# Two layers of a diffusion backbone on one core: another order of the expert blocks, and another end of the program

## The chip, the core and the metric

The kernel runs on one core of a Trainium2 chip. The core has five engines with a queue of instructions each: TensorE (PE, matmuls), VectorE (DVE), ScalarE (ACT), GpSimd (POOL) and SyncE (SP), which here issues the loads of the weights. They work on an on-chip memory (SBUF) and on eight banks in which matmuls sum (PSUM), and wait for each other through semaphores. The metric is the time of one execution in microseconds; the time of a kernel is the median of its runs.

## The reference

Two layers work on 256 latent tokens and 256 context tokens of width 1024, in float32. Each layer has a mixer (a gating MLP, a Fourier mix and windowed attention side by side) and a channel mixer. The first layer's channel mixer is a dense SwiGLU; the second layer's, for the 256 latent tokens alone, picks two of eight experts per token. This part is what the change is about:

```python
def moe_swiglu(y, w_r, b_r, wg, wu, wd):
    logits = (y @ w_r).astype(jnp.float32) + b_r.astype(jnp.float32)
    top_val, top_idx = lax.top_k(logits, TOP_K)
    gates = jax.nn.softmax(top_val, axis=-1)
    combine = jnp.sum(jax.nn.one_hot(top_idx, N_EXPERTS, dtype=jnp.float32)
                      * gates[..., None], axis=-2).astype(y.dtype)
    out = jnp.zeros_like(y)
    for e in range(N_EXPERTS):
        out = out + combine[..., e:e + 1] * swiglu(y, wg[e], wu[e], wd[e])
    return out
```

Behind it come a normalization of the sum, a multiplication by a gate and the addition to the tokens. Each expert has three matrices of 1024 x 3584, 44 MB in float32.

## The kernel before

The program is recorded by a planner in Python (`Sched`, L92). Work is written as tasks that yield an engine, the buffers they need and the events they wait for; at each step the planner takes the task that could start first by its own table of costs, and records its instructions. So the order on each engine, and the buffer that each tile gets, are fixed when the program is built. On the chip each engine runs its list in order.

In the expert stage a *unit* is one expert with a fixed number of token slots. Unit 0 is expert 0 with 32 slots (L44). The other seven experts are ranked on the chip by how many tokens chose them, and rank r gets `SLOTS[r]` slots: 160, 96, 96, 64, 64, 64, 32. Their weights are loaded through registers that hold the expert's number. An expert that gets more tokens than its unit has slots is served again by up to five overflow passes, each inside a branch (`moe_over`, L1639); the count of passes needed is read into a register of each engine. With the inputs at hand none is needed: the page of the profile lists 224 loads of each of the three kinds of expert weights, 28 for each of eight experts.

A unit has seven blocks of 512 hidden columns (`EB`). A block has 12 loads of 512 KB: four each of gate, up and down weights. The order of units and blocks is a table (L68); an entry is a rank (None for expert 0), the first block and the block behind the last:

```python
SEQ = ((None, 0, 7), (1, 0, 7), (3, 0, 7), (0, 0, 7), (4, 0, 7), (2, 0, 7), (5, 0, 7), (6, 0, 7))
```

`experts` (L1486) goes through it. `parts` (L1480) cuts a unit's slots into 128 rows, where there are so many, and a rest of 64 and 32. The 160-slot unit is the only one with a 128-row part. That part multiplies three times with weights that ScalarE and VectorE have split into a high and a low tile (`t_hi`, `t_lo`, `t_egu`, `t_edown`); the rests multiply with the loaded tile itself (`t_xgu`, `t_xdown`). Gathered tokens meet gate and up weights (128x512, 64x256 or 32x128 outputs), VectorE multiplies the two, TensorE transposes the product, and it meets the down weights (128x512, 64x512 or 32x512 outputs), whose sum stays in PSUM over all blocks of an entry of the table. Then a *flush* (`t_finish`, `t_xfinish`) splits the sum, multiplies it with the tokens' one-hot matrix and adds it, weighted, to two tiles `facc` of 128 tokens each.

Loads, split tiles and other tiles of this size share 41 slots of SBUF. The loads (`t_load`, L378) run ahead of TensorE as far as slots are free, less a reserve for everything that is no load. The reserve is a table too (L53): it starts at 8, and each pair sets it when the loads reach that block of the stage, counted from 0:

```python
REST = (8, ((20, 17), (27, 8)))
```

The unit of rank 0 holds blocks 21 to 27 of the stage. After the last unit's flush all engines meet the branch, and `fin` (L1866) takes the sum of squares of `facc` on ScalarE, multiplies `facc` by the gate on VectorE, and writes the result. All recorded instructions stand under L232 of the profile, the loads under L397, the branch under L1647.

Of the kernel before, what the change touches and what calls it, by code (L numbers as in the profile page):

```python
# [26 lines left out]
NE = 8  # L27
# [3 lines left out]
EPS = 1e-6  # L31
# [18 lines left out]
TABLE = 1.3  # L50
SC = {'PE': 1.0, 'ACT': 1.0, 'DVE': 1.0, 'POOL': 0.918, 'DMA': 1.0, 'NONE': 1.0}

REST = (8, ((20, 17), (27, 8)))  # L53
ORD = ((1, 0, 5, 6, 7, 4, 3, 2, 8, 9, 10, 11), (5, 3, 2, 4, 6, 7, 9, 10, 8, 11, 0, 1))
CAP = (3, 1, 2, 4)
ADB, HI0 = -0.7, 5
# [8 lines left out]
JO = (3, 6, 1, 2, 5, 7, 4, 0)  # L65
WO = ((0, 2), (0, 1, 2, 3), (0, 1, 2, 3, 4, 6))

SEQ = ((None, 0, 7), (1, 0, 7), (3, 0, 7), (0, 0, 7), (4, 0, 7), (2, 0, 7), (5, 0, 7), (6, 0, 7))  # L68


PE, ACT, DVE, POOL, DMA, NONE = "PE", "ACT", "DVE", "POOL", "DMA", "NONE"
# [214 lines left out]
class Core:  # L286
# [1159 lines left out]
            self.sc.rel(ht)  # L1446
        self.sc.set(out, acc)

    def t_finish(self, comb, acc, oht, last):

        fs = yield on(ACT, "sr:fs", "sr:fs", ev=[acc])
        for hf in range(2):
            c = slice(hf * 512, hf * 512 + 512)
            yield from self.g_split(acc.v[hf], fs[0][:, c], fs[1][:, c])
        self.sc.rel(*acc.v)
        yield on(PE, ev=[oht, self.combed, self.faccev])
        comb = comb()
        for t in range(2):
            for hf in range(2):
                c = slice(hf * 512, hf * 512 + 512)  # L1460
                p = yield on(PE, "b:m")
                o = oht.v[:, t * 128:t * 128 + 128]
                self.pe.matmul(p, o, fs[0][:, c], start=True, stop=False)
                self.pe.matmul(p, o, fs[1][:, c], start=False, stop=True)
                yield on(DVE)
                f = self.facc[t][:, c]
                self.v.scalar_tensor_tensor(f, p, comb[:, t:t + 1], f, op0=OP.mult, op1=OP.add)
                self.sc.rel(p)
        self.sc.rel(*fs)
        if last:  # L1470
            self.sc.rel(oht.v)
# [14 lines left out]
    def experts(self, units, seq):  # L1486
# [3 lines left out]
        for key, b0, b1 in seq:  # L1490
# [3 lines left out]
            for s, ws in parts:  # L1494
# [7 lines left out]
                acc = [Event() for _ in ws or [128]]  # L1502
                down.append((self.t_xdown(key, b0, b1, ws, hts, acc) if ws else self.t_edown(key, b0, b1, hts, acc[0]), 0.0))
                for i, w in enumerate(ws or [128]):
                    down.append(((self.t_xfinish if w == 64 else self.t_finish)(comb, acc[i], out[1][i], b1 == EB), -0.2))
            for b in range(b0, b1):
                for s, ws in parts:
                    out, hts = state[key, s]
# [130 lines left out]
    def moe_over(self):  # L1639

        tc, nc = self.tc, self.nc
        novf = nc.values_load(self.onum[0:1, MORE:MORE + 1], min_val=0, max_val=MORE)
        oidx = [nc.values_load(self.onum[0:1, i:i + 1], engines=(mybir.EngineType.SP,), min_val=0, max_val=NE - 1)
                for i in range(MORE)]

        def more(i):
            with tc.If(novf > i):  # L1647
                key = NE + i
                self.stream(self.moe_items([(key, 0, EB)], oidx[i]))
                self.experts({key: (key, lambda: self.otab[:, i, 0:2], 128, 128, lambda: self.otab[:, i, 2:4])}, [(key, 0, EB)])  # L1650
                self.sc.run()
                if i < MORE - 1:
                    more(i + 1)

        more(0)
# [209 lines left out]

    def fin(self):  # L1866

        def t():
            G, o = self.gate[1, 5, 0].v, []

            def mid():
                for t in range(2):
                    o.append((yield on(DVE, "s")))
                    self.v.tensor_mul(o[t], self.facc[t], G)

            rs = yield from self.g_rstd([[self.facc[t]] for t in range(2)], (), mid())
            for t in range(2):
                for hf in range(2):
                    c = slice(hf * 512, hf * 512 + 512)
                    self.v.scalar_tensor_tensor(o[t][:, c], o[t][:, c], rs[:, t:t + 1], self.h[t][:, c], op0=OP.mult, op1=OP.add)  # L1880
                    self.nc.sync.dma_start(self.out[t * 128:t * 128 + 128, c], o[t][:, c])

        self.sc.spawn(t())
        self.sc.run()


# [98 lines left out]
```

## Times and profile before

| | |
|---|---|
| median of three runs | 1733.65 us (1732.76 to 1735.01) |
| the profiled execution | 1729.91 us |
| its span, first to last instruction | 1728.0 us |
| TensorE busy | 1641.0 us (95%), 13276 matmuls |
| VectorE, ScalarE busy | 762.5 us (44%), 532.1 us (31%) |
| read from memory | 494.5 MB, 287 GB/s over the span |
| granted TensorE clock, mean | 0.982 |

The profile is of one execution, and its times are in microseconds from the span's start. The shares of the whole span mix stages: the first half computes the two mixers, the dense channel mixer and the router, and the expert stage runs from about 860 to 1715. The views used below are the slices of the span, stretches with the busy time of each engine and the rate of the loads, the waits of the queue that issues the loads, single instructions in order of time, and the instructions of one line.

### The profile page before, as it was taken

How to read it: one execution, taken by the hardware profiler on the slowest of the kernel's cores; microseconds unless marked ns; L12 is line 12 of the kernel's file. 1: busy time of each engine (PE TensorE's matmuls, PEld its weight loads, DVE VectorE, ACT ScalarE, POOL GpSimd, SP SyncE). 2: the span in 40 equal slices, each digit the busy share in tenths (PEclk: the TensorE clock that was granted, in tenths of full speed). 3: DMA queues.
4: the chain of work that ended last, by engine and by line, in shares of the span. 5: the costliest groups of instructions: out<-in, count | busy, mean ns of one | idle time of the engine just before them, and what ended most of it. 6: DMA issues, size and time to landing. Idle time of an engine off the chain costs nothing. (4 is left out here: it accounts for less than half of the span.)

```text
span 1728.0 us, 33043 instructions
## 1 busy us (share of the span) xinstructions
PE 1641.0 (95%) x13276; PEld 1144.2 (66%) x13276; DVE 762.5 (44%) x1402; ACT 532.1 (31%) x933; POOL 26.1 (2%) x49
## 2 busy tenths in 40 slices
PE   6999999999999999999989999999999999999865
PEld 3776889888888888886755555567776556545331
DVE  4566687664545467986313002165564010020102
ACT  3486453222223245547210001154452000000001
POOL 0100000000000020000000000000000000000000
PEclk9999999999999999999899999999999999999997
DMA  9506445644544465771899999999879999999995
GB/s 382 197 25 245 169 134 197 201 159 152 171 159 164 164 229 197 288 290 40 313 412 412 412 412 413 414 354 337 309 270 383 412 412 411 410 413 413 412 409 224
DMA packets 137888, 497.78 MB, mean 288 GB/s; under 512 B 16348, under 2 KB 16480, under 8 KB 137728
## 3 DMA queue, kind: packets, MB, share of 16 engines
q1 hardware_dynamic: 135072, 490.79, 74.6%
q0 software_dynamic: 1792, 4.18, 0.8%
q8 instruction: 106, 1.74, 0.4%
q10 hardware_dynamic: 864, 0.62, 0.1%
q14 instruction: 54, 0.44, 0.1%
HBM read 494.49 MB, written 1.05 MB: 287 GB/s over the span
## 5 line engine op out<-in xcount | busy, mean ns | idle before, releaser
L232 PE MATMUL b<-s,s 128*128 128x512 f32 (+3 forms) x6056 | 870.5, 344 | 9.6 <-DVE s L232 7.9
L232 PEld LDWEIGHTS b<-s,s 128*128 128x128 f32 (+2 forms) x6056 | 664.0, 157 | 182.5 <-issue 42.7
L232 PE MATMUL b<-s,f 128*32 128x128 f32 (+5 forms) x5472 | 526.9, 358 | 44.2 <-DMA s<-in_w_up_e_dram 12.5
L232 PEld LDWEIGHTS b<-s,f 128*32 128x32 f32 (+2 forms) x5472 | 321.2, 130 | 221.0 <-issue 84.1
L232 DVE TENSOR_TENSOR s<-s,s 128x1024 fp32r<-128x1024 f32 (+2 forms) x253 | 302.6, 1216 | 71.6 <-ACT s L232 56.4
L232 ACT ACTIVATE s<-s 128x1024 fp32r<-128x1024 f32 (+1 forms) x259 | 266.6, 1052 | 186.3 <-PE b L232 112.3
L232 DVE TENSOR_TENSOR f<-f,b 128x256 f32<-128x256 f32 (+3 forms) x91 | 39.1, 430 | 506.4 <-PE b L232 505.0
L232 ACT ACTIVATE f<-b 128x512 f32<-128x512 f32 (+3 forms) x161 | 77.8, 484 | 465.1 <-PE b L232 455.9
L232 PE MATMUL b<-s,q 128*32 128x512 f32 (+2 forms) x720 | 157.9, 592 | 3.2 <-DMA s<-in_w_down_e_dram 2.3
L232 DVE SCALAR_TENSOR_TENSOR s<-s,cs,s 128x1024 f32<-128x1024 f32 x73 | 91.8, 1280 | 42.6 <-DMA s<-in_w_ada_dram 42.5
L232 ACT ACTIVATE q<-b 128x128 f32<-128x128 f32 (+2 forms) x53 | 18.1, 342 | 275.1 <-PE b L232 263.8
L232 PEld LDWEIGHTS b<-s,q 128*32 128x32 f32 (+2 forms) x720 | 42.8, 128 | 74.0 <-issue 44.5
L232 DVE TENSOR_TENSOR s<-b,s 128x512 fp32r<-128x512 f32 (+2 forms) x77 | 48.6, 633 | 62.2 <-ACT s L232 38.4
L232 PE MATMUL b<-ident,f 128*128 128x128 f32 x313 | 57.5, 294 | 12.5 <-DVE f L232 7.8
L232 PEld LDWEIGHTS b<-ident,f 128*128 128x128 f32 x313 | 35.6, 144 | 50.4 <-DVE f L232 28.7
L232 ACT ACTIVATE s<-b 128x512 f32<-128x512 f32 (+3 forms) x99 | 50.2, 528 | 52.2 <-PE b L232 50.7
L232 ACT ACTIVATE f<-f 128x256 fp32r<-128x256 f32 x28 | 11.7, 419 | 116.3 <-DVE f L232 116.3
L232 DVE TENSOR_TENSOR f<-b,f 128x512 fp32r<-128x512 f32 x5 | 3.5, 692 | 89.7 <-ACT f L232 89.7
L232 PEld LDWEIGHTS b<-q,h 128*128 128x128 f32 x288 | 35.5, 201 | 9.3 <-issue 4.5
L232 PE MATMUL b<-q,h 128*128 128x64 f32 (+3 forms) x288 | 37.9, 288 | 1.9 <-DVE q L232 1.9
L232 DVE SCALAR_TENSOR_TENSOR s<-b,utab,s 128x512 f32<-128x512 f32 x40 | 28.5, 746 | 18.1 <-PE b L232 18.1
L232 ACT ACTIVATE f<-b,cols 128x256 f32<-128x256 f32 (+1 forms) x56 | 26.0, 555 | 33.5 <-PE b L232 29.9
(153 smaller groups left out, 560.4 us busy)
## 6 DMA issues: line engine op xcount, KB each, us to landing
s<-in_w_gate_e_dram SPq DMA_DIRECT2D x224, 512.0 KB, 10.0
s<-in_w_up_e_dram SPq DMA_DIRECT2D x224, 512.0 KB, 10.0
s<-in_w_down_e_dram SPq DMA_DIRECT2D x224, 512.0 KB, 10.0
s<-in_w_ada_dram SPq DMA_DIRECT2D x96, 512.0 KB, 4.5
s<-in_w_down_d_dram SPq DMA_DIRECT2D x56, 512.0 KB, 4.2
s<-in_w_gate_d_dram SPq DMA_DIRECT2D x28, 512.0 KB, 4.3
s<-in_w_up_d_dram SPq DMA_DIRECT2D x28, 512.0 KB, 3.4
s<-in_w_in_dram SPq DMA_DIRECT2D x24, 512.0 KB, 6.6
```

Source lines behind the costliest of these rows:

```text
L232: r = f(out, *a, **k)
```

## The change

The table of the order cuts the 160-slot unit into three entries (blocks 0 and 1, 2 and 3, 4 to 6) and puts a 64-slot unit behind each; the two 96-slot units follow, then the 32-slot unit. Each entry has sums and flushes of its own, so the 160-slot unit flushes three times. Its one-hot matrices and gathered tokens are kept from its first entry to its last. The table of the reserve has 17 from block 7 of the stage, the unit's first, to block 28, the first behind its last.

The branch before the overflow passes is told that its body is not the preferred path, so the passes stand on the taken side; the other path falls into a short block and jumps from there over the passes. And the last unit's flush is recorded behind the branch, in `fin`: its four additions each set an event, ScalarE squares each half of `facc` when its event is there, and VectorE multiplies by the gate between the additions.

```diff
@@ -50,7 +50,7 @@
 TABLE = 1.3
 SC = {'PE': 1.0, 'ACT': 1.0, 'DVE': 1.0, 'POOL': 0.918, 'DMA': 1.0, 'NONE': 1.0}
 
-REST = (8, ((20, 17), (27, 8)))
+REST = (8, ((7, 17), (28, 8)))
 ORD = ((1, 0, 5, 6, 7, 4, 3, 2, 8, 9, 10, 11), (5, 3, 2, 4, 6, 7, 9, 10, 8, 11, 0, 1))
 CAP = (3, 1, 2, 4)
 ADB, HI0 = -0.7, 5
@@ -65,7 +65,7 @@
 JO = (3, 6, 1, 2, 5, 7, 4, 0)
 WO = ((0, 2), (0, 1, 2, 3), (0, 1, 2, 3, 4, 6))
 
-SEQ = ((None, 0, 7), (1, 0, 7), (3, 0, 7), (0, 0, 7), (4, 0, 7), (2, 0, 7), (5, 0, 7), (6, 0, 7))
+SEQ = ((None, 0, 7), (0, 0, 2), (3, 0, 7), (0, 2, 4), (4, 0, 7), (0, 4, 7), (5, 0, 7), (1, 0, 7), (2, 0, 7), (6, 0, 7))
 
 
 PE, ACT, DVE, POOL, DMA, NONE = "PE", "ACT", "DVE", "POOL", "DMA", "NONE"
@@ -1446,7 +1446,7 @@
             self.sc.rel(ht)
         self.sc.set(out, acc)
 
-    def t_finish(self, comb, acc, oht, last):
+    def t_finish(self, comb, acc, oht, last, done=None):
 
         fs = yield on(ACT, "sr:fs", "sr:fs", ev=[acc])
         for hf in range(2):
@@ -1466,6 +1466,8 @@
                 f = self.facc[t][:, c]
                 self.v.scalar_tensor_tensor(f, p, comb[:, t:t + 1], f, op0=OP.mult, op1=OP.add)
                 self.sc.rel(p)
+                if done:
+                    self.sc.set(done[t][hf])
         self.sc.rel(*fs)
         if last:
             self.sc.rel(oht.v)
@@ -1502,7 +1504,12 @@
                 acc = [Event() for _ in ws or [128]]
                 down.append((self.t_xdown(key, b0, b1, ws, hts, acc) if ws else self.t_edown(key, b0, b1, hts, acc[0]), 0.0))
                 for i, w in enumerate(ws or [128]):
-                    down.append(((self.t_xfinish if w == 64 else self.t_finish)(comb, acc[i], out[1][i], b1 == EB), -0.2))
+                    finish, a = self.t_xfinish if w == 64 else self.t_finish, (comb, acc[i], out[1][i], b1 == EB)
+                    if (key, b0, b1) == seq[-1] and key < NE and (s, ws) == parts[-1] and i == len(ws or [128]) - 1:
+
+                        self.last = lambda done, f=finish, a=a: f(*a, done)
+                    else:
+                        down.append((finish(*a), -0.2))
             for b in range(b0, b1):
                 for s, ws in parts:
                     out, hts = state[key, s]
@@ -1644,7 +1651,7 @@
                 for i in range(MORE)]
 
         def more(i):
-            with tc.If(novf > i):
+            with tc.If(novf > i, preferred_fallthrough_block=False):
                 key = NE + i
                 self.stream(self.moe_items([(key, 0, EB)], oidx[i]))
                 self.experts({key: (key, lambda: self.otab[:, i, 0:2], 128, 128, lambda: self.otab[:, i, 2:4])}, [(key, 0, EB)])
@@ -1865,22 +1872,35 @@
 
     def fin(self):
 
-        def t():
-            G, o = self.gate[1, 5, 0].v, []
-
-            def mid():
-                for t in range(2):
-                    o.append((yield on(DVE, "s")))
-                    self.v.tensor_mul(o[t], self.facc[t], G)
-
-            rs = yield from self.g_rstd([[self.facc[t]] for t in range(2)], (), mid())
+        done = [[Event(), Event()] for _ in range(2)]
+        ss = self.fixed([128, 8], F32, "ss", 4)
+
+        def squares():
+            junk = yield on(ACT, "h")
+            for t in range(2):
+                for hf in range(2):
+                    yield on(ACT, ev=[done[t][hf]])
+                    i = 2 * t + hf
+                    self.s.activation(junk, self.facc[t][:, hf * 512:hf * 512 + 512], AF.Square, scale=1.0 / 32.0, accum_out=ss[:, i:i + 1])
+            self.sc.rel(junk)
+
+        def out(sq):
+            o = []
+            for t in range(2):
+                o.append((yield on(DVE, "s", ev=done[t])))
+                self.v.tensor_mul(o[t], self.facc[t], self.gate[1, 5, 0].v)
+            yield on(DVE, ev=[sq])
+            x, t, y = self.fixed([128, 4], F32, "rx", 2), self.fixed([128, 4], F32, "rt", 2), self.fixed([128, 4], F32, "ry", 6)
+            self.v.scalar_tensor_tensor(x[:, :2], ss[:, 0:4:2], EPS, ss[:, 1:4:2], op0=OP.add, op1=OP.add)
+            self.rsqrt(y[:, :2], x[:, :2], t[:, :2])
             for t in range(2):
                 for hf in range(2):
                     c = slice(hf * 512, hf * 512 + 512)
-                    self.v.scalar_tensor_tensor(o[t][:, c], o[t][:, c], rs[:, t:t + 1], self.h[t][:, c], op0=OP.mult, op1=OP.add)
+                    self.v.scalar_tensor_tensor(o[t][:, c], o[t][:, c], y[:, t:t + 1], self.h[t][:, c], op0=OP.mult, op1=OP.add)
                     self.nc.sync.dma_start(self.out[t * 128:t * 128 + 128, c], o[t][:, c])
 
-        self.sc.spawn(t())
+        self.sc.spawn(self.last(done))
+        self.sc.spawn(out(self.sc.spawn(squares())))
         self.sc.run()
 
 
```

The first place is on TensorE, at the down product of the 32-slot rest. Names: `b` are PSUM banks, `s` slots, `q` and `f` smaller tiles; the first number is the buffer's. Before, at the end of the 160-slot unit's second block:

```order
L232 MATMUL b0_10638<-s31_10530,q6_10543 32x512
L232 MATMUL b0_10638<-s26_10561,q6_10543 32x512
L232 MATMUL b0_10638<-s9_10583,q6_10543 32x512
L232 MATMUL b0_10638<-s24_10595,q6_10543 32x512
L232 MATMUL b5_10639<-s31_10530,q6_10543 32x512
L232 MATMUL b5_10639<-s26_10561,q6_10543 32x512
L232 MATMUL b5_10639<-s9_10583,q6_10543 32x512
L232 MATMUL b5_10639<-s24_10595,q6_10543 32x512
L232 MATMUL b7_10784<-ident_67,f8_10780 128x128
L232 MATMUL b4_10847<-s20_10793,f10_10005 32x128 x8
L232 MATMUL b4_10847<-s10_10819,f10_10005 32x128 x8
L232 MATMUL b1_10624<-s35_10373,s27_10455 128x512
```

The rows behind it (32x128 and 128x512) belong to later blocks of the same unit. After, at the end of the fourth block, which ends the second portion:

```order
L232 MATMUL b6_9926<-s19_9887,q0_10016 32x512
L232 MATMUL b6_9926<-s13_9905,q0_10016 32x512
L232 MATMUL b6_9926<-s37_9936,q0_10016 32x512
L232 MATMUL b6_9926<-s25_9942,q0_10016 32x512
L232 MATMUL b4_9927<-s19_9887,q0_10016 32x512
L232 MATMUL b4_9927<-s13_9905,q0_10016 32x512
L232 MATMUL b4_9927<-s37_9936,q0_10016 32x512
L232 MATMUL b4_9927<-s25_9942,q0_10016 32x512
L232 MATMUL b2_10092<-s0_9961,f5_9864 64x256 x4
L232 MATMUL b3_10100<-s27_10077,q1_8468 128x512
L232 MATMUL b3_10100<-s14_10078,q1_8468 128x512
L232 MATMUL b0_10038<-s31_9794,f5_9864 64x256 x4
```

Here the 64-slot unit follows (64x256), and between its rows the flush of the portion (128x512 with a `q`).

The second place is the queue of loads on SP. Before, these loads stand where slots `s9` and `s24` come free by the down product above (pieces 302 and 303 of the stage, counted from 0; the product's own are 280 to 283):

```order
L397 DMA s13_10878<-in_w_up_e_dram 128x1024
L397 ISA
L397 DMA s9_10900<-in_w_up_e_dram 128x1024
L397 ISA
L397 DMA s24_10910<-in_w_up_e_dram 128x1024
```

They are up weights of the same unit's fifth block. After, the loads that take the slots `s19`, `s13`, `s37` and `s25` of the second portion's last down product (pieces 220 to 223) are pieces 246 to 249:

```order
L397 DMA s19_10196<-in_w_down_e_dram 128x1024
L397 ISA
L397 DMA s13_10203<-in_w_down_e_dram 128x1024
L397 ISA
L397 DMA s37_10213<-in_w_gate_e_dram 128x1024
L397 ISA
L397 DMA s25_10221<-in_w_gate_e_dram 128x1024
L397 ISA
L397 DMA s0_10232<-in_w_gate_e_dram 128x1024
```

They are the last down weights of the 64-slot unit's second block and the gate weights of its fourth.

The third place is VectorE at the end. Before, the last unit's split, its four additions, and the branch:

```order
L232 TENSOR_TENSOR s_14843<-b_14281,s_14842 128x512
L232 TENSOR_TENSOR s_14843<-b_14282,s_14842 128x512
L232 SCALAR_TENSOR_TENSOR s_7885<-b_14848,utab,s_7885 128x512
L232 SCALAR_TENSOR_TENSOR s_7885<-b_14852,utab,s_7885 128x512
L232 SCALAR_TENSOR_TENSOR s_7886<-b_14856,utab,s_7886 128x512
L232 SCALAR_TENSOR_TENSOR s_7886<-b_14860,utab,s_7886 128x512
L1642 TENSOR_LOAD onum
L1647 COMPARE_AND_BRANCH
```

After, behind the branch (the first row is the end of the overflow passes):

```order
L1654 UNCONDITIONAL_BRANCH
L232 TENSOR_TENSOR s_20849<-b_14540,s_20848 128x512
L232 TENSOR_TENSOR s_20849<-b_14541,s_20848 128x512
L232 SCALAR_TENSOR_TENSOR s_7885<-b_20855,utab,s_7885 128x512
L232 SCALAR_TENSOR_TENSOR s_7885<-b_20859,utab,s_7885 128x512
L232 TENSOR_TENSOR s_20868<-s_7885,s_14693 128x1024
L232 SCALAR_TENSOR_TENSOR s_7886<-b_20864,utab,s_7886 128x512
L232 SCALAR_TENSOR_TENSOR s_7886<-b_20871,utab,s_7886 128x512
L232 TENSOR_TENSOR s_20877<-s_7886,s_14693 128x1024
L232 SCALAR_TENSOR_TENSOR rx<-ss 128x2
```

The two splits and four additions moved behind the branch, a multiplication by the gate stands behind each pair of additions, and the small instructions of the normalization follow. On TensorE the register load and the branch now stand between the last down product and the eight matmuls of the last addition. On the path without overflow each engine first brings its semaphore's count up to what it would be behind the passes and then jumps.

## Rows read from the trace of the kernel before

**Rows 1.** Slices of the span on the profile's page, 40 slices of 43.2 us, counted from 0.

```profile
PE   6999999999999999999989999999999999999865
GB/s 382 197 25 245 169 134 197 201 159 152 171 159 164 164 229 197 288 290 40 313 412 412 412 412 413 414 354 337 309 270 383 412 412 411 410 413 413 412 409 224
```

**Rows 2.** Three stretches of the expert stage; columns: us, busy by engine, PEclk, DMA share, GB/s.

```profile
860.00:1120.00 260.00, 247.01 (x3062) 143.39 (x3051) 39.67 (x137) 26.28 (x60) 1.84 (x2) 0.97 1.03 412
1140.00:1320.00 180.00, 179.64 (x1622) 127.77 (x1621) 112.06 (x118) 89.94 (x110) 0.00 (x0) 1.00 0.86 315
1340.00:1600.00 260.00, 257.25 (x2609) 143.09 (x2607) 28.53 (x61) 19.53 (x45) 0.00 (x0) 1.00 1.03 412
```

**Rows 3.** Waits of the issuing queue from 940 to 1120; us in total, times, longest.

```profile
SPq L397 <- PE b L232: 7.1, 26, 0.5
```

**Rows 4.** The same from 1140 to 1320.

```profile
SPq L397 <- PE b L232: 112.8, 73, 9.1
```

**Rows 5.** VectorE in time order, gate times up; start us, us, instruction, idle before.

```profile
1129.76 0.42 DVE L232 TENSOR_TENSOR f<-f,b 128x256 f32<-128x256 f32 x1 [4.45 <-PE b L232]
...
1159.74 0.68 DVE L232 TENSOR_TENSOR f<-f,b 128x512 f32<-128x512 f32 x1
...
1325.84 0.42 DVE L232 TENSOR_TENSOR f<-f,b 128x256 f32<-128x256 f32 x1 [0.27 <-PE b L232]
...
1376.82 0.42 DVE L232 TENSOR_TENSOR f<-f,b 128x256 f32<-128x256 f32 x1 [12.87 <-PE b L232]
...
1413.96 0.56 DVE L232 TENSOR_TENSOR f<-f,b 128x384 f32<-128x384 f32 x1 [4.19 <-PE b L232]
...
1538.48 0.42 DVE L232 TENSOR_TENSOR f<-f,b 128x256 f32<-128x256 f32 x1 [0.48 <-PE b L232]
```

**Rows 6.** DMA issues on the page; size of one, median us from issue to landing.

```profile
s<-in_w_gate_e_dram SPq DMA_DIRECT2D x224, 512.0 KB, 10.0
```

**Rows 7.** TensorE by form from 860 to 1728; busy us, mean ns.

```profile
L232 PE MATMUL b<-s,q 128*128 128x512 f32 x48 | 17.1, 441 | 0.3
```

**Rows 8.** VectorE by form from 1140 to 1320; columns as in group 7.

```profile
L232 DVE TENSOR_TENSOR s<-s,s 128x1024 fp32r<-128x1024 f32 x78 | 92.8, 1222 | 28.4 <-ACT s L232 25.6 <-PE b L232 1.8 <-DMA s<-in_w_gate_e_dram 0.2
...
L232 DVE SCALAR_TENSOR_TENSOR s<-b,utab,s 128x512 f32<-128x512 f32 x8 | 5.8, 744 | 0.6 <-PE b L232 0.6
```

**Rows 9.** VectorE around its overflow table, and a TensorE row, both in time order.

```profile
906.33 0.56 DVE L232 TENSOR_TENSOR s<-s,cols 128x384 f32<-128x384 f32 x1
...
915.32 0.17 DVE L232 CAST onum<-otab 128x6 int32<-128x6 f32 x1
...
928.81 1.90 PE L232 MATMUL b<-s,q 128*32 128x512 f32 x16
```

**Rows 10.** End of the program in order of time, all engines.

```profile
1710.15 0.60 ACT L232 ACTIVATE s<-b 128x512 fp32r<-128x512 f32 x1 [9.15 <-PE b L232]
...
1712.24 2.75 DVE L232 SCALAR_TENSOR_TENSOR s<-b,utab,s 128x512 f32<-128x512 f32 x4
...
1717.76 1.06 ACT L232 ACTIVATE s<-s 128x1024 f32<-128x1024 f32 x1 [6.16 <-DVEq L1647]
1717.98 2.36 DVE L232 TENSOR_TENSOR s<-s,s 128x1024 f32<-128x1024 f32 x2 [2.98 <-DVEq L1647]
...
1720.25 0.16 DVE L232 TENSOR_SCALAR rx<-ss 128x2 f32<-128x2 f32 x1
...
1722.22 2.74 DVE L232 SCALAR_TENSOR_TENSOR s<-s,ry,h 128x512 f32<-128x512 f32 x4
```

**Rows 11.** Instructions of the line with the branch; ns, first and last start us.

```profile
L1647 PEldq COMPARE_BRANCH  x1: 3575/3575/3575, 1713.0 to 1713.0; - x1
...
L1647 DVEq COMPARE_BRANCH  x1: 72/72/72, 1714.5 to 1714.5; - x1
...
L1647 DVEq EVENT_SEMAPHORE  x1: 21/21/21, 1717.5 to 1717.5; - x1
```

**Rows 12.** A stretch in the last unit, columns as in group 2.

```profile
1660.00:1680.00 20.00, 12.64 (x214) 7.25 (x218) 0.29 (x1) 2.03 (x5) 0.00 (x0) 1.00 1.02 405
```

## The prediction

> **What bounds the kernel now.** I read the slices first, counted from 0 [rows 1]. PE shows 9 tenths almost everywhere, but a busy PE is not a PE at its peak, so the row to read is the one of bytes: from slice 20 on (864 us) it stands at 412 GB/s, the rate of the weight loads at full flow, and sags only in slices 26 to 30 (354, 337, 309, 270, 383). The experts' weights are 672 loads of 512 KB; at 412 GB/s one takes 1.27 us, a block (12 loads) 15.3 us and an expert (7 blocks) 106.9 us. Measured by stretch [rows 2]: 412 before, 315 from 1140 to 1320, 412 after. At the full rate that stretch would have been 180 x (1 - 315/412) = 42.4 us shorter. Who holds the loads says the queue that issues them: from 940 to 1120 it waits 7.1 us in all for PE [rows 3]; from 1140 to 1320 it waits 112.8 us for PE [rows 4], that is for slots that PE has not read out. So the second half of the program runs at the speed of the loads, except around the 160-slot unit, where PE is 179.64 of 180 us busy and sets the pace.
>
> How far PE is too slow there is read from VectorE's gate-times-up multiplies, which mark each unit's blocks [rows 5]. First block of the 160-slot unit at 1159.74, of the next unit at 1325.84: 166.1 us, 23.7 a block against 15.3 of loading, 8.4 too many. The border into it (1129.76 to 1159.74, 30.0 us) holds deferred down products and the gather besides its block, 14.7 too many. The 64-slot unit behind it, border included, took 88.1 us (1325.84 to 1413.96), 18.8 less than its weights; a 96-slot unit 124.5 (1413.96 to 1538.48), 17.6 more.
>
> **The change part by part.** First the order of units. No weight is loaded twice and none dropped; the 160-slot unit runs as 2, 2 and 3 blocks, a 64-slot unit behind each. In the place of one long run in which PE falls behind there are three short ones, and what counts is how much of each the slots absorb. Now: 14.7 + 7 x 8.43 = 73.7 us too many, of which 42.4 were lost by the loads, so 31.3 were absorbed; 11.4 of them by nine slots (9 x 1.27) that the reserve's fall from 17 to 8 frees at that unit's last block.
>
> High end of the new loss: every portion pays its border and absorbs no more than now. Portions of two blocks: 14.7 + 16.9 = 31.6, and since the reserve stays at 17 there, 31.3 - 11.4 = 19.9 absorbed, 11.7 lost, twice. The third: 14.7 + 25.3 = 40.0; the reserve falls right behind it, so 31.3 absorbed, 8.7 lost. Together 32.
>
> Low end: nothing lost. The queue's rows in the section on the change show that, when PE has read the last down piece of the second portion (piece 223), loads up to piece 249 are let go, 26 ahead, where the end of the second block now lets go 20. Loads land 10.0 us after issue [rows 6], so some 8 of these are in flight; 18 pieces or 22.9 us are left against 16.9 of the two blocks, if the border's 14.7 belongs to the 64-slot unit before it, which has 18.8 to spare. For the third portion it is 30 pieces ahead, 28 us against 25.3.
>
> I take 20, nearer to the high end, since that is built from measured rows and the low one from the order alone. Gain: 42.4 - 20 = 22.4 us, between 10 and 42.
>
> The two additional flushes (the 128-row part and the 32-row part, twice) are 32 matmuls of 128x512. The 48 of that form took 17.1 us [rows 7], so 11.4 us of PE. They stand inside the 64-slot unit behind the portion, whose 18.8 us hide them; without that cover they would cost their 11.4. VectorE adds 16 additions of 0.74 us [rows 8], about 12 us, on an engine that is 112 of 180 us busy in its fullest stretch [rows 2]: nothing. The reserve of 17 over 21 blocks instead of 7 costs nothing while the loads wait for loads; its cost in the portions is in the sum.
>
> The first portion starts right behind the router. VectorE then splits its weights and its gathered tokens only behind the overflow table, which follows the 96-slot unit's tokens (ready at 906.9) and ends at 915.5 [rows 9]; five splits of 1.22 us [rows 8] come next, the first of the tokens among them, so the first matmul comes at about 922, 15 later. Bounds: 0 to 15 us. I take 0: in PE's new order the down product of expert 0's last block, which waits for its weights until 928.81 [rows 9], stands among the portion's first matmuls and holds them anyway.
>
> Now the end. Today the last unit's sums are split from 1710.15, added up from 1712.24 to 1714.99, and then everything waits for the branch: the squares start at 1717.76, the gate multiplies at 1717.98, the chain of ten small instructions at 1720.25, and the final multiplies end at 1724.96 [rows 10]. The branch row of VectorE starts at 1714.5 and its next instruction at 1717.5; on PE the branch lasts 3.6 us [rows 11]. After the change VectorE and ScalarE branch while PE still multiplies. But PE now meets its branch between its last down product and the matmuls of the last addition. ScalarE's split waits only for a count that PE sets before it leaves the branch, so about 1710.2 stays. If PE needs its 3.6 us from there, its matmuls start at 1713.8; an addition comes two matmuls of 0.36 (17.1 by 48 [rows 7]) and some 0.1 behind them, at 1714.7. Four additions (2.75 as now) and the two gate multiplies between them (2.36 as now) end at 1719.8, and the square of the last half (half of 1.06) ends before that, since only a gate multiply of 1.2 lies behind the last addition. The small chain and the final multiplies take 4.7 from first to last: 1724.5, 0.4 us earlier than now. If PE passes the branch without that pause, the additions stay at 1712.24 and the end comes at 1722.1, 2.9 earlier. I take 0.4, since PE's own row is the one at hand.
>
> [...]
>
> Sum: -22.4 - 0.4 = -22.8 us. The profiled execution took 1729.91 us (span 1728.0), so 1707.1; the runs' median lies 3.7 above it, so **1710.9 us** in runs, rounded to 1711.
>
> **The rivals.** (a) The slots cover all of it: loss near 0, 1691 us. For it: 26 pieces ahead. Against it: in the present unit the slots did not cover even the first blocks, since the rate sags from 1140 on.
>
> (b) PE is late at the end. The two 96-slot units now follow each other, 17.6 us over their weights each, 35 together, on top of what the border brings; the 32-slot unit behind them has to win it back. There PE is busy 12.64 of 20 us [rows 12], so it wins at most 37% of 107, 39 us. If it starts more than 39 late, what is left, or what the slots then refuse to the loads, is some 8 us: 1719 us.
>
> (c) The loss moves and does not shrink: three borders where one was, each with its own sag, and the sags sum to 38 to 46: no change, about 1734.
>
> (d) Slower. What the first portion took out of the slots is not refilled before the second. Each 64-slot unit has 18.8 to spare and the slots have to get back 19.9, so this decides as soon as the spare falls clearly below that, for instance because the flush (5.7) and the conversion of the next portion's weights delay it. With half won back (9.4) the second portion absorbs 19.9 - 10.5 and loses 22.2, the third 31.3 - 10.5 and loses 19.2; with the first, 53.1: 10.7 more than now, 1744 us. Against it: after the present unit, with a lateness of the same size, PE waits again for loads within six blocks (the gap to the mark at 1376.82).
>
> **How the numbers follow.** This kernel's measurement can tell 0.2% (3.5 us) from no change. Forecast (loss 10 to 32, 1700 to 1723): 0.55. (a) with a loss under 10: 0.13. (b): 0.15. (c): 0.08. (d): 0.09. So faster 0.83, same 0.08, slower 0.09. The forecast's own range is 1700 to 1723. For 8 in 10 I reach to 1695, part of the way into (a), and up to 1727, past (b), and leave the rest of (a), (c) and (d) outside.
>
> **What would show it.** Right: around each portion the rate dips for at most 10 us worth of loading; between the portions the issuing queue waits for loads again; the sag's sum falls from 42 to about 20; PE pauses some 3 us between its last down product and the matmuls of the last addition, and the last load lands some 22 us earlier. Wrong: no dip at all (a); the queue still waiting for PE, or PE not waiting for loads, in the last unit (b); dips that grow from portion to portion (d); a dip at 925 to 960 larger than the others, which would put a price on the overflow table in front of the first portion.

## The result and the profile after

| | before | after |
|---|---|---|
| median of the runs compared | 1733.20 us (1730.21 to 1735.01) | 1709.63 us (1707.21 to 1712.03) |
| ratio, 95% interval | | 0.9866 [0.9845, 0.9886] |
| the profiled execution | 1729.91 us | 1710.48 us |
| its span | 1728.0 us | 1708.6 us |

The median is 23.6 us lower (1733.20 - 1709.63), the profiled span 19.4 (1728.0 - 1708.6). The difference lies in the executions: the profiled one of before was 3.3 us under the median of this table, the one of after 0.9 over it. The account below is of the 19.4 us.

The row of bytes on the page of after, to be laid beside [rows 1] (40 slices, now of 42.7 us):

```profile
GB/s 370 203 38 235 161 136 215 180 164 144 193 153 159 172 203 200 284 264 130 246 367 392 329 414 413 400 409 414 412 352 413 413 412 412 414 412 397 391 411 228
```

The deep valley of slices 26 to 30 is gone. In its place are a dip in slice 22 (329), a smaller one in 29 (352), a shallow one in 25 (400) and two faint ones near the end (397, 391). Measured by stretch, with the columns of [rows 2]:

```profile
920.00:980.00 60.00, 57.06 (x518) 42.70 (x519) 37.19 (x52) 23.58 (x33) 0.00 (x0) 0.95 0.90 339
1100.00:1120.00 20.00, 20.00 (x206) 14.97 (x207) 7.40 (x10) 5.48 (x9) 0.00 (x0) 1.00 0.98 374
1140.00:1320.00 180.00, 179.78 (x1466) 110.86 (x1461) 65.62 (x80) 51.10 (x73) 0.00 (x0) 1.00 1.01 399
1240.00:1280.00 40.00, 40.00 (x311) 28.97 (x311) 21.62 (x27) 15.88 (x21) 0.00 (x0) 1.00 0.95 348
1560.00:1600.00 40.00, 40.00 (x531) 23.70 (x523) 3.64 (x11) 2.84 (x6) 0.00 (x0) 1.00 0.99 376
1640.00:1680.00 40.00, 31.89 (x593) 18.13 (x582) 1.15 (x4) 3.41 (x10) 0.00 (x0) 0.97 1.03 412
```

A portion is one of the three entries that the 160-slot unit is cut into, and the loss of a stretch is the time by which it would have been shorter at 412 GB/s. It is 60 x (1 - 339/412) = 10.6 us at the first portion, 1.8 at the second, 6.2 at the third and 3.5 at 1560 to 1600, where the two 96-slot units run: 22.1 us, where the kernel before lost 42.4. The stretch that held the 160-slot unit before runs at 399 instead of 315. Who holds the loads is again told by the waits of the issuing queue (us in total, times, longest); the first row is from 900 to 1010, around the first portion, the other two from 1010 to 1085, in the 64-slot unit behind it:

```profile
SPq L397 <- PE b L232: 36.9, 30, 5.8
...
SPq L397 <- DMA s<-in_w_gate_e_dram: 14.2, 20, 0.8
...
SPq L397 <- PE b L232: 4.4, 14, 0.7
```

Around the portion the queue waits for PE, as in [rows 4]; behind it mostly for earlier loads (14.2 us on one of three kinds), and for PE 4.4 us, as in [rows 3]. So a 64-slot unit does give the slots back before the next portion.

### The profile page after: what moved, and what is told of

Its sections match the earlier page's. It is cut to its first block, busy times and chain, and to the rows that moved or that the text cites. A ratio compares the mean times of both kernels' runs of the same rounds, so it can differ in the third digit from the quotient of the medians.

```text
span 1708.6 us, 33100 instructions
## 1 busy us (share of the span) xinstructions
PE 1635.1 (96%) x13308; PEld 1146.5 (67%) x13308; DVE 778.1 (46%) x1426; ACT 536.1 (31%) x945; POOL 26.1 (2%) x49
## 5 line engine op out<-in xcount | busy, mean ns | idle before, releaser
L232 PE MATMUL b<-s,f 128*32 128x128 f32 (+5 forms) x5472 | 520.6, 355 | 29.2 <-DVE ones L632 8.6
L232 ACT ACTIVATE f<-b 128x512 f32<-128x512 f32 (+4 forms) x161 | 77.6, 483 | 425.8 <-PE b L232 424.8
L232 PE MATMUL b<-s,q 128*64 128x512 f32 (+2 forms) x752 | 161.0, 587 | 6.0 <-issue 4.5
L232 PEld LDWEIGHTS b<-s,q 128*64 128x64 f32 (+2 forms) x752 | 47.5, 132 | 74.3 <-issue 53.4
L232 DVE TENSOR_TENSOR s<-b,s 128x512 fp32r<-128x512 f32 (+2 forms) x85 | 53.8, 638 | 80.0 <-ACT s L232 57.3
L232 ACT ACTIVATE s<-b 128x512 fp32r<-128x512 f32 (+3 forms) x107 | 54.6, 533 | 86.5 <-PE b L232 75.3
L232 PEld LDWEIGHTS b<-ident,f 128*128 128x128 f32 x313 | 35.0, 143 | 41.8 <-DVE f L232 22.4
L232 DVE SCALAR_TENSOR_TENSOR s<-b,utab,s 128x512 f32<-128x512 f32 x56 | 40.8, 748 | 42.1 <-PE b L232 42.0
L232 PEld LDWEIGHTS b<-q,h 128*128 128x128 f32 x288 | 35.6, 200 | 5.7 <-issue 2.4
L232 PE MATMUL b<-q,h 128*128 128x32 f32 (+3 forms) x288 | 36.9, 284 | 0.8 <-DVE q L232 0.8
L232 ACT ACTIVATE f<-b,cols 128x256 f32<-128x256 f32 (+1 forms) x56 | 25.9, 555 | 34.4 <-PE b L232 31.3
```

The lines of the kernel that those rows point to most:

```text
L232: r = f(out, *a, **k)
```

## The experiments

Each ran beside the kernel before on the same chip; a ratio below is to that. Changes that one edit makes at several places are cut to their core. The name in brackets is the one that the texts use for the run; *before* and *after* are the two kernels. From the last weights to the end means from the start of the down product that they release to the end of the final multiplies.

**The order alone** (order_alone). The kernel before with the two tables changed, and nothing else:

```diff
-REST = (8, ((20, 17), (27, 8)))
+REST = (8, ((7, 17), (28, 8)))
-SEQ = ((None, 0, 7), (1, 0, 7), (3, 0, 7), (0, 0, 7), ...
+SEQ = ((None, 0, 7), (0, 0, 2), (3, 0, 7), (0, 2, 4), ...
```

> The kernel before with the changed order table and reserve table alone; branch and end as before. Theory (the order brings the whole gain, the new end gives a little back: in the changed kernel 16.8 us lie between the release by the last weights and the end of the final multiplies, 15.9 before): loads' loss about 22 us, 15.9 us at the end, 1709 us or 0.9 us under the changed kernel. Rival (the new end earned part of the 23 us): 1711 to 1713 us, 1 to 3 above the changed kernel.

1706.93 us, ratio 0.9864 [0.9839, 0.9889]: the whole gain, against 0.9866 for the full change. Its loads lose some 25 us, 3 more than expected, and its end is that of before. In order of time, TensorE's last down product, the split and the additions:

```profile
1686.41 4.75 PE L232 MATMUL b<-s,q 128*32 128x512 f32 x18 [0.17 <-SPq L1647]
...
1687.49 0.60 ACT L232 ACTIVATE s<-b 128x512 fp32r<-128x512 f32 x1 [8.64 <-PE b L232]
...
1689.59 2.75 DVE L232 SCALAR_TENSOR_TENSOR s<-b,utab,s 128x512 f32<-128x512 f32 x4
```

**The end alone** (tail_alone). The changed kernel with the two tables of before.

> The changed kernel with the old order and the old reserve: branch and end new. Theory: the loads lose 42 us as before; from the last weights to the end of the final multiplies 16.8 us instead of 15.9, span 1728.9, time about 1 us above before, TensorE standing about 3.7 us between its last down product and the matmuls of the last addition. Prediction's own term: 0.4 to 2.9 us under before.

1732.63 us, 1.0017 [1.0002, 1.0033]: not faster, and slower by an amount at the edge of what the runs resolve. The same rows of its trace, with the matmuls of the last addition:

```profile
1709.37 1.90 PE L232 MATMUL b<-s,q 128*32 128x512 f32 x10 [0.21 <-SPq L1654]
...
1711.45 1.08 ACT L232 ACTIVATE s<-b 128x512 fp32r<-128x512 f32 x2 [9.80 <-PEq L1654]
...
1715.26 3.75 PE L232 MATMUL b<-s,q 128*128 128x512 f32 x8 [3.99 <-issue]
1716.49 1.60 DVE L232 SCALAR_TENSOR_TENSOR s<-b,utab,s 128x512 f32<-128x512 f32 x2 [3.13 <-PE b L232]
```

The split starts 2.1 us behind the last down product's start (1711.45 - 1709.37), where order_alone has 1.1, and TensorE stands 3.99 us ahead of the last matmuls. From that product's start to the end of the final multiplies it is 17.2 us; before it was 15.9.

**The branch laid out as before** (branch_default). One line undone in the changed kernel:

```diff
-            with tc.If(novf > i, preferred_fallthrough_block=False):
+            with tc.If(novf > i):
```

> The changed kernel with the branch laid out as before (no preference stated), the last flush still behind it. Theory (TensorE pays for whichever jump leads over the passes): it still stands 3.3 to 3.7 us between its last down product and the matmuls of the last addition, 16.8 to 17.2 us from the last weights to the end of the final multiplies, 1708 to 1711 us. Rival (the layout matters): the pause falls under 1 us or grows by 1 us or more.

1708.52 us, 0.9877 [0.9857, 0.9896]: no difference from the full change that the runs resolve. Its TensorE branch (count, duration in ns, then first and last start):

```profile
L1654 PEldq COMPARE_BRANCH  x1: 3522/3522/3522, 1688.0 to 1688.0; - x1
L1654 PEldq EVENT_SEMAPHORE  x1: 51/51/51, 1691.6 to 1691.6; - x1
```

It takes 3.5 us, and the count that ScalarE waits for is set only behind it. TensorE stands 3.1 us between the last down product and the matmuls of the last addition, and it is 16.5 us from that product to the end: both a little under what was expected, and the 16.5 at the lower edge of what the new layout's runs show (16.3 to 17.3). The layout of the branch earned nothing that can be told from zero.

**The unit in one piece, at the place of the first portion** (whole_first).

```diff
+REST = (8, ((7, 17), (14, 8)))
+SEQ = ((None, 0, 7), (0, 0, 7), (3, 0, 7), (4, 0, 7), (5, 0, 7), (1, 0, 7), (2, 0, 7), (6, 0, 7))
```

> The changed kernel with the 160-slot unit in one piece, first behind expert 0, and then the three 64-slot units; reserve 17 over its seven blocks alone. Theory (splitting with 64-slot units between earns the gain): 14.7 + 7 x 8.43 us too many as before and some 8 us for the overflow table ahead of it, less the 27 us that the changed kernel's first portion absorbed (39.6 too many, 12.4 lost) and 11 at its end: 44 to 55 us lost there, 3.5 late, 1735 to 1746 us. Rival (it is the place behind expert 0 that earns it): 1707 to 1715 us.

1739.74 us, 1.0044 [1.0027, 1.006], as the theory had it. The place behind expert 0 earns nothing by itself; the stretch of the unit:

```profile
920.00:1120.00 200.00, 198.57 (x1765) 142.56 (x1767) 123.31 (x138) 94.25 (x117) 0.00 (x0) 0.98 0.87 310
```

200 x (1 - 310/412) = 49.5 us lost, 7 more than in the kernel before. Whether cutting the unit is enough, or the 64-slot units between the portions are needed, the next run tells.

**The portions without cover** (no_cover). The same with portions (0, 0, 2), (0, 2, 4), (0, 4, 7) in a row.

> As whole_first, but the 160-slot unit in its three portions, one right behind the other: the two additional flushes stand between portions and not inside 64-slot units. Theory (the 64-slot units hide the flushes and give the slots back): the 11.4 us of TensorE for the flushes come on top of whole_first, 8 to 15 us above it. Rival (a flush fits beside other work anyway): within 4 us of whole_first.

1744.97 us, 1.0074 [1.0051, 1.0097], 5.2 us above whole_first: between the two expectations. The stretch of the three portions:

```profile
920.00:1120.00 200.00, 197.87 (x1737) 142.28 (x1739) 134.61 (x155) 97.13 (x122) 0.00 (x0) 0.99 0.83 298
```

200 x (1 - 298/412) = 55.3 us are lost. So cutting the unit gains nothing by itself: what gains is a 64-slot unit behind each portion. The gate-times-up multiply of the first 64-slot unit comes 8.8 us later than there (1125.87 instead of 1117.12), so most of the 11.4 us of flushes does delay TensorE; why the loads lose only some 5 of it is not settled.

**The reserve of before, with the new order** (old_reserve). `REST = (8, ((20, 17), (27, 8)))` in the changed kernel.

> The changed kernel with the reserve table of before (17 from block 20 of the stage to 27, 8 elsewhere), so that the loads of the first two portions leave 8 slots free. Theory (the split weights need the slots): the portions run slower than the 11 to 15 us a block of the changed kernel, the first two sags grow by 5 to 15 us together, 1714 to 1724 us. Rival (nine more loads ahead absorb more): first two sags smaller, 1700 to 1706 us. No part in it: 1709 us.

1710.38 us, 0.9876 [0.9853, 0.9898]. The stretches of the first and the third portion:

```profile
920.00:980.00 60.00, 57.75 (x522) 43.27 (x523) 36.51 (x51) 22.12 (x31) 0.00 (x0) 0.96 0.90 335
1240.00:1280.00 40.00, 40.00 (x311) 29.04 (x306) 21.50 (x26) 15.54 (x20) 0.00 (x0) 1.00 0.94 350
```

335 and 350 against 339 and 348: in the new order the reserve has no part in it. Both theories on it fall.

**A 96-slot unit ahead of the first portion** (unit96_first), one instead of two behind the last: `(1, 0, 7), (0, 0, 2), (3, 0, 7), (0, 2, 4), (4, 0, 7), (0, 4, 7), (5, 0, 7), (2, 0, 7)`, with the reserve moved along.

> The changed kernel with one 96-slot unit before the first portion (one instead of two behind the last), the reserve of 17 moved with the portions (blocks 14 to 34). Theory (the first portion's sag of about 10.6 us is so large because the overflow table stands in front of its splits; the sag of 3.5 us at 1560 to 1600 comes from two 96-slot units in a row): first portion's sag 4 to 7, late sag under 1, 1701 to 1704 us. Rival 1 (the first sag has nothing to do with the table): 1706 us. Rival 2 (the 96-slot unit's lateness of 17.6 us is carried into the first portion): sag there 15 or more, 1712 us.

1725.78 us, 0.9966 [0.995, 0.9981]: some 16 us worse than the change, and my theory on the first portion was wrong; rival 2 named the mechanism and priced it too low. The first portion, and the stretch late in the stage:

```profile
1020.00:1100.00 80.00, 80.00 (x716) 48.24 (x716) 42.03 (x54) 30.38 (x39) 0.00 (x0) 1.00 0.78 282
1540.00:1600.00 60.00, 60.00 (x808) 35.85 (x806) 4.19 (x12) 3.83 (x8) 0.00 (x0) 1.00 1.03 412
```

At the portion 80 x (1 - 282/412) = 25.2 us are lost; late there is nothing, so the 3.5 us there do come from two 96-slot units in a row. A unit that is itself late by 17.6 hands most of that lateness to the portion behind it (25.2 - 10.6 = 14.6).

**The overflow table later** (table_later). In the changed kernel, VectorE's table waits for the third block of the first 64-slot unit:

```diff
-        yield on(DVE)
+        yield on(DVE, ev=[self.late])
         self.overflow(w[:, :208].rearrange("p (j k) -> p j k", k=16))
...
+            if key == 4 and b0 == 0:
+                self.late = hts[2]
```

> The changed kernel with VectorE's overflow table held back until the third block of the first 64-slot unit. Theory (the table in front of the first portion costs): the portion's first product is marked 5 to 8 us earlier than 943.2, its sag falls from 10.6 to about 5, 1704 us. Rival (TensorE is held there by the down product of expert 0's last block, as the prediction took it): the mark and the sag stay, 1709 to 1710 us.

1699.54 us (1696.26 to 1701.51), 0.9827 [0.9801, 0.9853], the lowest median of all that ran. It is 10 us under the full change, which was measured apart from it; by the ratios to the kernel before (0.9827 against 0.9866) it is some 7, and the two intervals just overlap. VectorE at the start of the first portion, first after, then table_later (start, duration, instruction, idle before):

```profile
907.69 0.29 DVE L232 TENSOR_TENSOR f<-f,b 128x128 f32<-128x128 f32 x1 [8.23 <-PE b L232]
907.92 0.16 DVE L232 TENSOR_SCALAR f<-rank 128x7 f32<-128x7 f32 x1
...
916.41 0.17 DVE L232 CAST onum<-otab 128x6 int32<-128x6 f32 x1
916.52 5.77 DVE L232 TENSOR_TENSOR s<-s,s 128x1024 fp32r<-128x1024 f32 x5
922.20 0.68 DVE L232 TENSOR_TENSOR s<-f,s 128x512 fp32r<-128x512 f32 x1
...
943.24 0.68 DVE L232 TENSOR_TENSOR f<-f,b 128x512 f32<-128x512 f32 x1
```

```profile
902.32 0.29 DVE L232 TENSOR_TENSOR f<-f,b 128x128 f32<-128x128 f32 x1 [8.13 <-PE b L232]
...
907.01 0.69 DVE L232 TENSOR_TENSOR s<-f,s 128x512 fp32r<-128x512 f32 x1 [2.48 <-ACT s L232]
...
910.58 8.03 DVE L232 TENSOR_TENSOR s<-s,s 128x1024 fp32r<-128x1024 f32 x7
...
923.19 0.69 DVE L232 TENSOR_TENSOR f<-f,b 128x512 f32<-128x512 f32 x1 [4.05 <-PE b L232]
```

In after the table's instructions run from 907.92 to 916.6, then five weight splits, then the first split of tokens at 922.20. In table_later both splits of tokens are done by 907.7. The portion's first gate multiply follows expert 0's last by 20.9 us (923.19 - 902.32) instead of 35.6 (943.24 - 907.69). The stretches of table_later:

```profile
920.00:980.00 60.00, 59.96 (x552) 40.23 (x550) 34.89 (x46) 22.24 (x32) 0.00 (x0) 1.00 1.01 397
1100.00:1120.00 20.00, 20.00 (x136) 10.19 (x130) 7.48 (x11) 2.94 (x6) 0.00 (x0) 1.00 1.03 416
1220.00:1260.00 40.00, 40.00 (x381) 29.23 (x369) 25.30 (x33) 18.25 (x25) 0.00 (x0) 1.00 0.92 340
1540.00:1580.00 40.00, 40.00 (x579) 25.90 (x579) 3.64 (x11) 2.83 (x6) 0.00 (x0) 1.00 1.00 381
```

The first portion loses 2.2 us in the place of 10.6, the second nothing, the third 7.0, and 3.0 remain late: more than the theory had. (In the two profiled executions the first gate multiply of expert 0 stands at 862.7 and at 857.8, and from there table_later is 9.2 us shorter.)

The edit does more than move the table. The planner fixes the order from its own costs, and without the table it records more of the portion's matmuls ahead of the down product of expert 0's last block. TensorE in table_later, that product in the last row:

```profile
913.02 8.44 PE L232 MATMUL b<-s,s 128*128 128x512 f32 x36
...
923.91 1.90 PE L232 MATMUL b<-s,q 128*32 128x512 f32 x16
```

Here 48 of the portion's gate and up matmuls stand ahead of the product (6 before the first row, its 36, and 6 between the rows); in after it is 12. What the table's time is worth apart from this order was not tried.

**Both together** (old_end_late), order_alone with the later table:

> order_alone (the new order with the branch and the end of before) with the overflow table held back as in table_later. Theory (the two effects add): the loads lose 12 to 13 us before the end, 15.9 us from the last weights to the end of the final multiplies, 0.9 to 1.3 under table_later, 1698 to 1699 us, ratio to before 0.980 to 0.982. Rival (order_alone lost 25 us and not 22, so its other end also moves the loads): equal to table_later or above.

1701.56 us (1695.96 to 1707.66), 0.9836 [0.9811, 0.9861]. 16.1 us at the end, as expected, but the loads run at 368, 366 and 387 GB/s from 940 to 980, 1220 to 1280 and 1540 to 1600 and lose 4.3, 6.7 and 3.6 us there, 14.6 where 12 to 13 were expected. The time can't be told from table_later's: a microsecond is under what these runs resolve. Against order_alone (0.9864) the later table is worth some 5 us here.

**Portions of three, two and two blocks** (split322_late), on old_end_late: `(0, 0, 3)`, `(0, 3, 5)`, `(0, 5, 7)`.

> old_end_late with portions of three, two and two blocks. Theory (each portion finds about 31 us of loads in its slots, whatever the reserve, and pays 14.7 us for its border and 8.43 a block): the loss of a three-block portion, 8.7 by this working, moves from the third portion to the first, 8 to 11 us at 920 to 980 and under 2 at the third; time within 2 us of old_end_late. Rival (the first portion starts with fuller slots and covers three blocks): the third sag goes without another coming, 5 us under old_end_late.

1701.39 us, 0.9836 [0.9815, 0.9857], the time of old_end_late. The first and the third portion:

```profile
940.00:1000.00 60.00, 60.00 (x561) 41.34 (x553) 31.03 (x42) 20.23 (x29) 0.00 (x0) 1.00 0.93 346
1220.00:1280.00 60.00, 59.64 (x518) 39.10 (x516) 34.20 (x46) 22.40 (x30) 0.00 (x0) 1.00 1.03 413
```

The first loses 9.6 us now, where old_end_late lost 4.3, and the third none, where that lost 6.7: the loss went with the third block, as the theory has it.

**The branch ahead of the 32-slot unit** (branch_early_late), on table_later. The last unit's loads, its work and the last flush are recorded behind the branch (the edit also sets the reserve to 17 for the passes and back to 8 behind them):

```diff
-        moe = self.moe_items(self.seq())
+        moe = self.moe_items(self.seq()[:-1])
...
+        self.stream(self.moe_items(self.seq()[-1:]))
+        self.experts(self.units, self.seq()[-1:])
         self.sc.spawn(self.last(done))
```

> table_later, and the branch with the overflow passes moved ahead of the 32-slot unit, whose loads and work are recorded behind it with the last flush. Theory (in the changed kernel the branch costs TensorE 3.7 us and ScalarE's split 0.8 us on the path from the last weights to the end; ahead of the 32-slot unit it lies where TensorE has time left): 16.9 us at the end become 12 to 13, 1695 us. Rival (the drained border ahead of the branch and the loads behind SP's own branch cost more than that): 1700 us or more.

1745.47 us, 1.0077 [1.0054, 1.01]. The end is as short as expected, 13.1 us from the last product, but ahead of the unit the loads all but stop: 232, 1, 2 and 356 GB/s in the four stretches of 20 us from 1560, 51 us lost. What the issuing queue waited for between 1560 and 1640, and the rows of the branch:

```profile
SPq L397 <- DVEq L1658: 42.4, 1, 42.4
```

```profile
L1658 SPq COMPARE_BRANCH  x2: 38/46/53, 1571.2 to 1574.6; - x2
...
L1658 DVEq EVENT_SEMAPHORE  x1: 21/21/21, 1620.0 to 1620.0; - x1
```

SP passed the branch by 1574.6, and then its first load stood 42.4 us until VectorE reached the branch and brought its count up at 1620.0. That a count at the branch was waited for is shown; that it is because the passes, had they run, would have used the load's slot is the likely reason, and was not tried apart.

## Why the prediction came out right, and where it did not

**The bound and the main term held.** The loss of the loads was to fall from 42.4 to 20 and fell to 22.1; the product that the last weights release started at 1688.85 instead of 1709.06, 20.2 earlier against 22.4 forecast. Its row before:

```profile
1709.06 4.74 PE L232 MATMUL b<-s,q 128*32 128x512 f32 x18 [0.36 <-SPq L1647]
```

The order brings the gain without the end (order_alone, tail_alone) and whatever the reserve (old_reserve). Within the order neither the place (whole_first) nor the cutting by itself (no_cover) brings it; the portions need a unit with time to spare behind each.

**The closeness of the total is in part luck.** For the runs 1711 was forecast and 1709.63 measured; for the profiled execution 1707.1 was forecast and 1710.48 measured, 3.4 more. Executions of one kernel differ by that much: those of before lie between 1730.21 and 1735.01.

**But the 20 was made of wrong parts.** Three steps of its high end failed, and the first two nearly cancelled.

First, the 31.3 us that the slots absorb were cut to 19.9 for the first two portions, because 11.4 were put down to the reserve's fall. old_reserve shows that the reserve does nothing in the new order. With 31.3 throughout, the prediction's own border and blocks give 31.6 - 31.3 = 0.3 for a portion of two blocks and 40.0 - 31.3 = 8.7 for three: 9.3 in all. table_later, where the table doesn't stand ahead of the portions, lost 2.2, 0 and 7.0: 9.2. old_end_late, with the same order of units, lost 4.3 at the first and 6.7 at the third, 11.0, so the agreement holds to some 2 us and not to 0.1. split322_late moved the loss of the third portion to the first.

Second, the overflow table in front of the first portion was priced at 0 out of 0 to 15, since the down product of expert 0's last block was thought to wait for its weights until 928.81 and to hold the portion's matmuls anyway. The row [rows 9] names no wait; it only stands there in the order. The queue takes the gate and up weights of a block ahead of the down weights of the block before it. By this the product's weights were issued by 913.5 in before, and with 10.0 us to landing [rows 6] they were there some 5 us ahead of it. In after the product stands behind the portion's first 12 matmuls, and those waited for VectorE. The queue's loads of the product's weights, and TensorE in order of time:

```profile
912.03 4.05 SPq L397 DMA_DIRECT2D s<-in_w_down_e_dram  x4
...
914.38 0.47 PE L232 MATMUL b<-s,s 128*128 128x512 f32 x1
917.80 0.50 PE L232 MATMUL b<-s,s 128*128 128x512 f32 x1 [2.95 <-DVE s L232]
922.94 4.24 PE L232 MATMUL b<-s,s 128*128 128x512 f32 x10 [4.64 <-DVE s L232]
927.11 1.92 PE L232 MATMUL b<-s,q 128*32 128x512 f32 x16
```

TensorE stood 2.95 and 4.64 us for VectorE's splits, and reached the product at 927.11 without a wait. But the premise was not idle: the last of the product's weights, issued at 915.75 with 10.1 us to landing, were there at 925.9, so in this order the product would have held TensorE until then even without the table. table_later shows that the product need not stand there: with the table moved the planner put it behind 48 matmuls, and the first portion lost 8.4 us less. The step that failed is the price of 0; how much of the 8.4 is VectorE's time and how much the order that comes with it stays open. The text had named a larger dip at 925 to 960 as the sign of a price on the table, and it was there.

Third, rival (b), 35 us of lateness from two 96-slot units, came true in part: 3.5 us at 1560 to 1600 instead of 8, a figure that it gave without a working, and the last unit won the rest back (PE 31.89 of 40 us busy from 1640 to 1680). Of the four stretches' 22.1 us, 9.2 are the portions' own, some 8.4 go with the table and 3.5 are this; the remaining 1 is not assigned. By old_end_late the first part would be 11.0 and the second 6.3.

**The end was mis-sized, with the wrong sign.** -0.4 was forecast; after took 16.8 us from the start of the last down product to the end of the final multiplies, before 15.9 [rows 10]: +0.9, and tail_alone +1.3. Its rows in after, and those of the branch:

```profile
1688.85 1.90 PE L232 MATMUL b<-s,q 128*32 128x512 f32 x10 [0.18 <-SPq L1654]
...
1690.93 1.08 ACT L232 ACTIVATE s<-b 128x512 fp32r<-128x512 f32 x2 [9.64 <-PEq L1654]
...
1694.46 3.64 PE L232 MATMUL b<-s,q 128*128 128x512 f32 x8 [3.70 <-issue]
1695.58 1.61 DVE L232 SCALAR_TENSOR_TENSOR s<-b,utab,s 128x512 f32<-128x512 f32 x2 [2.73 <-PE b L232]
...
1702.90 2.74 DVE L232 SCALAR_TENSOR_TENSOR s<-s,ry,h 128x512 f32<-128x512 f32 x4
```

```profile
L1654 DVEq COMPARE_BRANCH  x2: 51/53/55, 1680.8 to 1681.0; - x2
...
L1654 PEldq COMPARE_BRANCH  x2: 95/1719/3343, 1689.5 to 1690.9; - x2
...
L1654 PEldq EVENT_SEMAPHORE  x1: 51/51/51, 1690.8 to 1690.8; - x1
```

The failed step is "about 1710.2 stays". 1710.2 was the moment when half of the product was done; ScalarE now waits for the count that TensorE sets behind all of it, so its split starts 2.1 us behind the product's start instead of 1.1, and TensorE's pause begins that much later too. This is 1.0 of the 1.3 us that the sum missed. The pause itself was right: 3.6 forecast, 3.70 measured. The compare takes 95 ns and the jump behind the count 3343: the jump over the passes is what costs, and either layout has such a row on TensorE's path (3522 ns in branch_default). No run shows TensorE past the branch without a pause, as an end 2.9 us earlier would have needed: it stood 3.70 us here, 3.99 in tail_alone and 3.10 in branch_default. Why its jump takes that long was not shown. VectorE's jump, by contrast, lies 10 us ahead of its next work (1681.0 and 1691.56) and costs nothing now; TensorE's decides.

**The other rivals.** (a), that the slots cover all of it, fell by the dips. (c), a loss that only moves, fell by the sum. (d), no refill between portions, fell by the second portion: 1.8 us lost, and the queue waiting for loads ahead of it. Its mechanism is real all the same: unit96_first shows it, with a unit in front that has nothing to spare and 25.2 us lost at the portion.

## What to carry to other kernels

Where a stream of loads is the bound, cut a slower stretch into pieces that the buffers can absorb, and put a stretch with time to spare behind each: here that took the loss from 42.4 us to 22.1, cutting alone gained nothing (55.3 lost in no_cover, 49.5 in whole_first), and a stretch that was late itself cost the piece behind it 14.6 us. Count as border all work that stands in front of a piece on the helping engines (the overflow table's 8.7 us on VectorE here), and read a row without a named wait as order, not as waiting. In this program work put behind a branch waited for a count that stands behind the whole list of the engine ahead of it and not for the one product it needs (ScalarE's split came 2.1 us behind the product's start in the place of 1.1), and the jump that cost time was TensorE's, which came to the branch last, whichever way it was laid out (3.3 us in after, 3.5 in branch_default).

## What was not expected of the hardware

A load recorded behind the branch waited 42.4 us in branch_early_late, until VectorE had brought its count up there, though no pass ran. And VectorE's row of the branch didn't show its price: in before it lists 72 ns [rows 11] with 3.0 us to the next instruction, and in branch_default 72 ns with 5.6 (1679.3 to 1684.9), while TensorE's row carries the pause itself (3343 ns in after, 3522 in branch_default, 3575 before).
